# Eight experts instead of six norm their own rows in a hybrid encoder's mixture of experts; tiles, norms and slot finding placed elsewhere

## The chip, the core and the metric

The kernel is one program on one core of a Trainium2 chip. Its engines are TensorE (PE in the profile; PEld are its weight loads), VectorE (DVE), ScalarE (ACT), GpSimd (POOL) and SyncE (SP), each with its own queue of instructions that it works off in order; they meet through semaphores. SP and POOL issue the DMAs here. The metric is the device time of one execution in microseconds (us), lower is better.

## The reference

One layer of an encoder over 1024 tokens of width 1024: an input norm, one projection, three mixers side by side (retention, a state-space model, windowed attention), an output projection, a residual norm; then a mixture of experts and a last residual norm. The change lies in the last two:

```python
def expert_choice_ffn(x, router_w, w_gate, w_up, w_down):
    cap = EC_FACTOR * seq // N_EXPERTS                  # 128 tokens for each of 16 experts
    aff = jax.nn.softmax(einsum('bld,de->ble', x, router_w), axis=-1)
    gates, idx = lax.top_k(jnp.swapaxes(aff, 1, 2), cap)
    xs = x[bidx, idx]
    hdn = silu(xs @ w_gate) * (xs @ w_up)               # 1024 -> 2048, per expert
    out = (hdn @ w_down) * gates[..., None]             # 2048 -> 1024
    return jnp.zeros_like(x).at[bidx, idx].add(out)
h = layer_norm(ALPHA * h + expert_choice_ffn(h, ...), ln2_g, ln2_b)
```

Each expert takes its own 128 tokens, so a token can be in several experts or in none, and its row is complete when the last expert that has it has been added. Everything is float32; a product of two float32 operands is made of three matmuls on a high and a low part of each ("splits").

## The kernel before

**The expert stage.** Everything up to the router comes first; from about 505 us on, `Experts.quarter(q)` runs for q from 0 to 64. Expert e has the quarters 4e to 4e + 3, numbered f = 0 to 3. A quarter has six steps s, each one unit of weights of 1 MB: steps 0 and 1 multiply the tokens `xT` by a quarter of the gate matrix into `gu`, steps 2 and 3 by a quarter of the up matrix, and steps 4 and 5 multiply the hidden rows `hT` of the quarter before by the down matrix into `y`. A step is 12 matmuls on TensorE.

**The weights.** `load` (L1851) brings a unit from HBM into one of five raw buffers `wraw`; ScalarE rounds it to the high part of `whl` (L1858, `high`), VectorE subtracts that from the raw values to make the low part (L1865, `low`), which frees the raw buffer, and `low` at once issues the load of the unit five further on. After each step's matmuls the program has ScalarE and VectorE make the unit six steps ahead (`lead`), so both run some steps ahead of TensorE, but in program order with everything else on their queues.

**The hidden rows.** ScalarE takes the silu of the gate product after step 2 (L1894), VectorE multiplies by the up product after step 3 (L1900, `hid`), and TensorE transposes `hid` at the opening of the next quarter (L1803, `tp<-ident,hid`); ScalarE and VectorE split the result into `hT`. TensorE's transpose of `hid` thus stands behind every piece of work that VectorE has before L1900 in its queue.

**The order of the work around it** is written by hand. `at(self.before, q, s, fn)` and `at(self.after, q, s, fn)` hang a function before or after step s of quarter q; functions of one place run in the order in which they were hung there. `plan(q)` hangs those of quarter q, among them the slots and rows of the next expert: `expert_hot` (two comparisons on VectorE, L1770), `expert_slots` (eight small matmuls on TensorE, L1779), `expert_gather` (four tiny VectorE instructions and, issued by POOL, the gather `xs` of the expert's 128 rows from `h1_d`, L1792), and two halves of transposes of `xs`, split into `xT`.

**Summing and norming.** `acc_d` in HBM starts as the residual. The first experts, e < E - LAST, add their 128 rows to it with a scatter that adds (`expert_add`, L2022 and L2023). From e = E - LAST on, an expert gathers its rows of `acc_d` ahead (`final_rows`, L2041, into `eo`), adds its product to them on VectorE (`last_sum`, L2104), scatters the sums back (L2123), norms them (`last_mean` L2059 on ScalarE, L2060 on POOL; `last_var` L2066 on ScalarE, L2067 and L2068 on POOL; `last_gain` L2072 and `last_shift` L2076 on VectorE) and scatters them into the output (`last_scatter`, L2109); `last_norm` hangs this in the second quarter of the following expert, and expert 15 does it at the end (`last_rows`). For tokens that no such expert has, `final_norm` loads each of the eight tiles of 128 tokens of `acc_d` (`zz`, L2086 on SP), norms it with the same functions and stores it (L2089). Rows that an own-norm expert scatters later overwrite those of the tile; the order of the stores and scatters is kept by dependencies.

Of the kernel before, what the change touches and what calls it, by code (L numbers as in the profile page):

```python
# [20 lines left out]
P = 128  # L21
# [8 lines left out]
NEG = -1e30  # L30
TWO_PI = 6.283185307179586
PI_LO = 3.1415925
LAST = 6


def bcast(ap, n):
# [60 lines left out]
class Plan:  # L97
# [5 lines left out]
    def at(self, place, fn):  # L103
        self.items.append((place, len(self.items), fn))
# [1660 lines left out]
def expert_hot(K, e):  # L1765

    hot = []
    for t0 in range(0, NT, 4):
        hot.append(K.ex.tile([P, 4, P], BF16, name="hot", bufs=2))
        K.nc.vector.tensor_tensor(hot[-1], K.slot[:, t0:t0 + 4, e:e + 1].to_broadcast([P, 4, P]),  # L1770
                                  K.slots[:, None, :].to_broadcast([P, 4, P]), OP.is_equal)
    return hot


def expert_slots(K, e, hot):

    pt = K.ptp.tile([P, 4, P], F32, name="tp")
    for t in range(NT):
        K.nc.tensor.matmul(pt[:, 0, 0:5], hot[t // 4][:, t % 4, :], K.tok[:, t, e, :], start=(t == 0), stop=(t == NT - 1))  # L1779
    return pt  # L1780


def expert_gather(K, e, pt):

    nc, pool = K.nc, K.ex
    c = pool.tile([P, 6], F32, name="slotc", bufs=2)
    nc.vector.tensor_copy(c[:, 0:5], pt[:, 0, 0:5])
    nc.vector.tensor_tensor(K.index[:, e:e + 1], c[:, 0:1], c[:, 1:2], OP.add)
    xs = None
    if e:  # L1790
        xs = pool.tile([P, D], F32, name="xs", bufs=3)
        nc.gpsimd.indirect_dma_start(out=xs, out_offset=None, in_=K.h1_dram,  # L1792
                                     in_offset=bass.IndirectOffsetOnAxis(ap=K.index[:, e:e + 1], axis=0))
    nc.vector.tensor_tensor(c[:, 5:6], c[:, 3:4], c[:, 4:5], OP.add)
    nc.vector.tensor_tensor(K.gates[:, e:e + 1], c[:, 5:6], c[:, 2:3], OP.add)
    return xs
# [26 lines left out]
class Experts:  # L1823
# [59 lines left out]
    def plan(self, q):  # L1883

        K, nc, pool = self.K, self.K.nc, self.K.ex
        e, f = divmod(q, 4)
        at, box = self.at, {}

        def put(name, fn):
            return lambda: box.__setitem__(name, fn())  # L1890

        def silu():
            self.h[q] = pool.tile([P, 512], F32, name="hid", bufs=2)
            nc.scalar.activation(self.h[q], self.pg[q][0], AF.Silu)  # L1894

        def hidden():
            self.hT[q] = [pool.tile([P, 4, P], F32R, name=f"hT{s}", bufs=2) for s in range(2)]
            split(K, *self.hT[q], box["tp"])
        at(self.after, q, 2, silu)
        at(self.after, q, 3, lambda: nc.vector.tensor_tensor(self.h[q], self.h[q], self.pg[q][1], OP.mult))  # L1900
        s = 0 if q < 4 * E - 1 else 4
        at(self.before, q + 1, s, put("tp", lambda: turned(K, self.h[q], 0)))
        at(self.after if s == 0 else self.before, q + 1, s, hidden)
        if f == 0 and e + 1 < E:
            late = ((q, 0), (q, 3), (q, 3), (q + 2, 1)) if e else ((q + 2, 3), (q + 2, 4), (q + 2, 4), (q + 3, 3))
            at(self.after, *late[0], put("hot", lambda: expert_hot(K, e + 1)))
            at(self.before, *late[1], put("pt", lambda: expert_slots(K, e + 1, box["hot"])))
            at(self.after, *late[2], put("xs", lambda: expert_gather(K, e + 1, box["pt"])))
            for half in range(2):
                q1, s1 = late[3][0], late[3][1] + half  # L1910
                at(self.before, q1, s1, put(half, lambda half=half: turned(K, box["xs"], half * 4)))
                at(self.after, q1, s1, lambda half=half: self.tokens(e + 1, half, box[half]))
        if f == 0:
            if e < E - LAST:
                at(self.after, q + 5, 0, lambda: expert_add(K, e, self.py[e]))
            elif e < E - 1:
                last_norm(self, e)
        if q == 4 * (E - LAST):
            at(self.after, q, 1, lambda: final_consts(K, self.I))
            for t, n in enumerate((2, 3, 6, 10, 11, 14, 18, 22)):  # L1920
                final_norm(self, t, q + n)
        if q >= 4 * (E - LAST) and f == 0:
            at(self.after, q + 1, 3, lambda: final_rows(K, e))

# [132 lines left out]
def last_mean(K, z, junk, s):  # L2057

    K.nc.scalar.activation(junk, z, AF.Copy, accum_out=s[:, 0:1])  # L2059
    K.nc.gpsimd.tensor_scalar(s[:, 1:2], s[:, 0:1], -1.0 / D, None, op0=OP.mult)  # L2060


def last_var(K, z, junk, s):

    nc = K.nc
    nc.scalar.activation(junk, z, AF.Square, bias=s[:, 1:2], accum_out=s[:, 2:3])  # L2066
    nc.gpsimd.tensor_scalar(s[:, 3:4], s[:, 2:3], 1.0 / D, EPS, op0=OP.mult, op1=OP.add)  # L2067
    nc.gpsimd.tensor_tensor(s[:, 4:5], s[:, 3:4], K.mhalf[:, 0:1], OP.pow)  # L2068
# [10 lines left out]
def final_norm(X, t, q):  # L2079

    K, b = X.K, {}

    def load():
        zz = K.raw0.tile([P, 2, D], F32, name="zz", tag="wraw")
        b["z"], b["y"], b["s"] = zz[:, 0, :], zz[:, 1, :], stats_tile(K)
        K.nc.sync.dma_start(b["z"], K.acc_dram[t * P:(t + 1) * P, :])  # L2086

    def store():
        ins = K.nc.sync.dma_start(X.O["out"][t * P:(t + 1) * P, :], b["y"])  # L2089
        write_out(K, ins, K.scatters[-1:])  # L2090
        K.tiles.append(ins)
    X.at(X.after, q - 1, 5, load)
    X.at(X.after, q, 3, lambda: last_mean(K, b["z"], b["y"], b["s"]))
    X.at(X.after, q, 4, lambda: last_var(K, b["z"], b["y"], b["s"]))
    X.at(X.after, q + 1, 0, lambda: last_gain(K, b["z"], b["y"], b["s"]))
    X.at(X.after, q + 1, 1, lambda: last_shift(K, b["y"], b["s"]))
    X.at(X.after, q + 1, 2, store)


def last_sum(K, e, py, z):  # L2100
# [15 lines left out]
def last_norm(X, e):  # L2116

    K, b, q = X.K, {}, 4 * e + 5

    def total():  # L2120
        b["z"], b["s"] = K.last, stats_tile(K)
        last_sum(K, e, X.py[e], b["z"])
        K.nc.gpsimd.indirect_dma_start(out=K.acc_dram, in_=b["z"], in_offset=None,  # L2123
                                       out_offset=bass.IndirectOffsetOnAxis(ap=K.index[:, e:e + 1], axis=0))

    def mean():
        b["y"] = K.raw0.tile([P, 2, D], F32, name="yl", tag="wraw")[:, 0, :]
        last_mean(K, b["z"], b["y"], b["s"])

    def shift():  # L2130
        last_shift(K, b["y"], b["s"])
        last_scatter(K, X.O, e, b["y"])
    X.at(X.after, q, 0, total)
    X.at(X.after, q, 1, mean)
    X.at(X.after, q, 2, lambda: last_var(K, b["z"], b["y"], b["s"]))
    X.at(X.after, q, 3, lambda: last_gain(K, b["z"], b["y"], b["s"]))
    X.at(X.after, q, 4, shift)


def last_rows(X, e):  # L2140
# [205 lines left out]
```

## Time and profile before

| | us |
|---|---|
| timed runs | 1651.81, 1662.2, 4021.71; median 1662.2 |
| the profiled execution | 1650.03, of which the span from first to last instruction is 1648.3 |
| expert stage | from about 505 to the end |
| quarters 41 to 62, in which experts norm their own rows | from 1215.3 to 1613.2 |

The profile is of one execution on the core; its granted TensorE clock was 0.988 of full speed over the span. One of the timed runs (4021.71) lies far off the two others. A row of the order of time reads: start in us, how long, engine, line, operation, output <- inputs, and in brackets how long the engine was idle before and who ended that. In the rows a group of instructions has its count behind an x. Instructions that only issue a DMA or wait are not counted as busy.

### The profile page before, as it was taken

How to read it: one execution, taken by the hardware profiler on the slowest of the kernel's cores; microseconds unless marked ns; L12 is line 12 of the kernel's file. 1: busy time of each engine (PE TensorE's matmuls, PEld its weight loads, DVE VectorE, ACT ScalarE, POOL GpSimd, SP SyncE). 2: the span in 40 equal slices, each digit the busy share in tenths (PEclk: the TensorE clock that was granted, in tenths of full speed). 3: DMA queues.
4: the chain of work that ended last, by engine and by line, in shares of the span. 5: the costliest groups of instructions: out<-in, count | busy, mean ns of one | idle time of the engine just before them, and what ended most of it. 6: DMA issues, size and time to landing. Idle time of an engine off the chain costs nothing.

```text
span 1648.3 us, 21108 instructions
## 1 busy us (share of the span) xinstructions
PE 1571.1 (95%) x7704; PEld 1290.9 (78%) x7704; DVE 1415.7 (86%) x1734; ACT 1128.8 (68%) x1272; POOL 212.5 (13%) x237
## 2 busy tenths in 40 slices
PE   7999998899988999999999999999999999999997
PEld 5888887687776788888888888888887788777785
DVE  7986863777789989998898988989889998999996
ACT  4644544865746678777777777777768777786773
POOL 4002110011010010110101101011011304131221
PEclk9999999899999999999999999999999999999999
DMA  5566475425128999999999999999999999999993
GB/s 191 188 169 144 111 232 184 131 77 160 52 95 323 345 373 413 411 367 392 371 392 389 367 394 371 395 386 371 394 384 395 399 390 400 386 418 381 373 404 155
DMA packets 102682, 505.74 MB, mean 307 GB/s; under 512 B 12977, under 2 KB 28081, under 8 KB 51890
## 3 DMA queue, kind: packets, MB, share of 16 engines
q1 hardware_dynamic: 87426, 476.60, 75.3%
q0 software_dynamic: 15152, 27.79, 6.1%
q8 instruction: 60, 0.98, 0.2%
q14 instruction: 44, 0.36, 0.1%
HBM read 461.36 MB, written 42.99 MB: 306 GB/s over the span
## 4 chain that ended last, share of the span: by engine, by line
PE 61%; DVE 14%; DMA 10%; issue 7%; ACT 6%; POOL 1%; SPq 0%; POOLq 0%; DVEq 0%; ACTq 0%
PE gu L1818 26%; PE y L1818 13%; DVE whl L1865 6%; PE mm L79 4%; PE mm L81 4%; PE mm L80 4%; DMA zz<-acc_d 4%; DMA wraw<-in_exp_w_down 3%; ACT whl L1858 3%; DMA wraw<-in_exp_w_gate 2%; PE tp L1803 2%; PE po L1362 1%; ACT S L1336 1%; DVE pT L71 1%; PE sm L1462 1%
## 5 line engine op out<-in xcount | busy, mean ns | idle before, releaser
L1865 DVE TENSOR_TENSOR whl<-wraw,whl 128x2048 fp32r<-128x2048 f32 x384 | 873.0, 2288 | 90.4 <-ACT whl L1858 87.4
L1858 ACT ACTIVATE whl<-wraw 128x2048 fp32r<-128x2048 f32 x384 | 734.6, 1918 | 235.5 <-PE gu L1818 81.0
L1818 PE MATMUL gu<-whl,xT 128*128 128x512 f32 x3072 | 732.3, 395 | 0.0
L1818 PEld LDWEIGHTS gu<-whl,xT 128*128 128x128 f32 x3072 | 571.1, 189 | 117.2
L1818 PE MATMUL y<-whl,hT 128*128 128x512 f32 x1536 | 359.1, 389 | 0.7 <-ACT hT L70 0.7
L1818 PEld LDWEIGHTS y<-whl,hT 128*128 128x128 f32 x1536 | 288.2, 188 | 60.6 <-ACT hT L70 0.9
L1792 POOL DMA_INDIRECT xs<-h_d,index x15 | 41.4, 2759 | 732.7 <-PE y L1818 544.4
L79 PE MATMUL mm<-hT,whl 128*128 128x512 f32 x160 | 66.0, 412 | 0.0
L70 ACT ACTIVATE hT<-tp 128x512 fp32r<-128x512 f32 x80 | 45.9, 583 | 27.4 <-PE tp L178 14.1
L80 PE MATMUL mm<-hT,whl 128*128 128x512 f32 x160 | 62.7, 392 | 0.0
L81 PE MATMUL mm<-hT,whl 128*128 128x512 f32 x160 | 62.6, 391 | 0.0
L1803 PE MATMUL tp<-ident,hid 128*128 128x128 f32 x256 | 39.6, 278 | 21.3 <-DVE hid L1900 21.3
L71 DVE TENSOR_TENSOR hT<-tp,hT 128x512 fp32r<-128x512 f32 x80 | 54.0, 683 | 5.0 <-ACT hT L70 4.9
L1803 PEld LDWEIGHTS tp<-ident,hid 128*128 128x128 f32 x256 | 30.9, 141 | 33.5 <-DVE hid L1900 27.3
L79 PE MATMUL mm<-WO,yh 128*128 128x512 f32 x128 | 51.7, 404 | 3.4 <-ACT yh L70 3.4
L80 PE MATMUL mm<-WO,yh 128*128 128x512 f32 x128 | 50.3, 393 | 0.0
L81 PE MATMUL mm<-WO,yl 128*128 128x512 f32 x128 | 48.9, 392 | 0.0
L79 PE MATMUL mm<-whl,hT 128*128 128x512 f32 (+1 forms) x128 | 46.7, 365 | 0.1
L1336 ACT ACTIVATE S<-S,asm 128x384 f32<-128x384 f32 (+1 forms) x64 | 36.9, 578 | 13.0 <-DVE asm L1323 7.6
L81 PE MATMUL mm<-whl,hT 128*128 128x512 f32 (+1 forms) x128 | 44.3, 346 | 1.4 <-DVE hT L71 1.4
L80 PE MATMUL mm<-whl,hT 128*128 128x512 f32 (+1 forms) x128 | 44.4, 347 | 0.5 <-DVE whl L135 0.5
L1900 DVE TENSOR_TENSOR hid<-hid,gu 128x512 f32<-128x512 f32 x64 | 43.5, 680 | 1.1 <-PE gu L1818 1.0
(428 smaller groups left out, 1780.1 us busy)
## 6 DMA issues: line engine op xcount, KB each, us to landing
wraw<-in_exp_w_gate SPq DMA_DIRECT2D x128, 1024.0 KB, 7.9
wraw<-in_exp_w_up SPq DMA_DIRECT2D x128, 1024.0 KB, 8.0
wraw<-in_exp_w_down SPq DMA_DIRECT2D x128, 1024.0 KB, 8.3
wraw<-in_w_in SPq DMA_DIRECT2D x8, 1024.0 KB, 7.1
x<-in_x SPq DMA_DIRECT2D x8, 512.0 KB, 4.4
h_d<-x SPq DMA_DIRECT2D x8, 512.0 KB, 3.1
q_d<-kst SPq DMA_DIRECT2D x32, 128.0 KB, 2.5
wraw<-in_w_out SPq DMA_DIRECT2D x4, 1024.0 KB, 6.1
```

The costliest lines, as they stand in the source:

```text
L70: nc.scalar.activation(hi, src, AF.Copy)
L71: eng.tensor_tensor(lo, src, hi.bitcast(F32), OP.subtract)
L79: nc.tensor.matmul(ps, a[0], b[0], start=start, stop=False)
L80: nc.tensor.matmul(ps, a[0], b[1], start=False, stop=False)
L81: nc.tensor.matmul(ps, a[1], b[0], start=False, stop=stop)
L1336: nc.scalar.activation(S[g][:, :W], S[g][:, :W], AF.Exp, bias=nm[:, g:g + 1], accum_out=rs[:, g:g + 1])
L1792: nc.gpsimd.indirect_dma_start(out=xs, out_offset=None, in_=K.h1_dram, in_offset=bass.IndirectOffsetOnAxis(ap=K.index[:, e:e + 1], axis=0))
L1803: K.nc.tensor.transpose(pt[:, c, :], src[:, (c0 + c) * P:(c0 + c + 1) * P], K.ident)
L1818: nc.tensor.matmul(ps, a[s][c], u[:, t, i * w:(i + 1) * w], start=first and id(ps) not in began, stop=last and left[id(ps)] == 0)
L1858: self.K.nc.scalar.activation(u[:, 0, :], self.raw[k1].rearrange("p a b -> p (a b)"), AF.Copy)
L1865: self.K.nc.vector.tensor_tensor(u[:, 1, :], raw, u[:, 0, :].bitcast(F32), OP.subtract)
L1900: at(self.after, q, 3, lambda: nc.vector.tensor_tensor(self.h[q], self.h[q], self.pg[q][1], OP.mult))
```

## The change

Five things are done.

1. `LAST` goes from 6 to 8: experts 8 and 9 norm their own rows too, so eight do (8 to 15), and eight add (0 to 7).
2. The eight token tiles are normed one in each expert from 8 on, in its third and fourth quarters. Before, they stood at quarters 42, 43, 46, 50, 51, 54, 58 and 62 (two experts had two, and the adding ones none).
3. In each tile's norm the load moves from step 5 of the quarter before to step 0, the mean from step 3 to step 5, the variance from step 4 to step 0 of the next quarter, gain, shift and store one step later each.
4. In an own-norm expert's norm the mean goes from step 1 to 2, variance from 2 to 3, gain from 3 to 4, shift from 4 to 5.
5. Experts 1 to 7 find in their third quarter also the slots of expert e + 8 (9 to 15). Those experts' rows are then gathered (`expert_rows`, new) without the slot work in the quarter of the gather, at the place where they were gathered before.

```diff
-LAST = 6
+LAST = 8
...
+def expert_rows(K, e):
+
+    xs = K.ex.tile([P, D], F32, name="xs", bufs=3)
+    K.nc.gpsimd.indirect_dma_start(out=xs, out_offset=None, in_=K.h1_dram,
+                                   in_offset=bass.IndirectOffsetOnAxis(ap=K.index[:, e:e + 1], axis=0))
+    return xs
...
-    xs = None
-    if e:
-        xs = pool.tile([P, D], F32, name="xs", bufs=3)
...
+    xs = expert_rows(K, e) if rows else None
...
-            at(self.after, *late[0], put("hot", lambda: expert_hot(K, e + 1)))
-            at(self.before, *late[1], put("pt", lambda: expert_slots(K, e + 1, box["hot"])))
-            at(self.after, *late[2], put("xs", lambda: expert_gather(K, e + 1, box["pt"])))
+            if e < E - LAST:
+                at(self.after, *late[0], put("hot", lambda: expert_hot(K, e + 1)))
+                at(self.before, *late[1], put("pt", lambda: expert_slots(K, e + 1, box["hot"])))
+                at(self.after, *late[2], put("xs", lambda: expert_gather(K, e + 1, box["pt"], True)))
+            else:
+                at(self.after, *late[2], put("xs", lambda: expert_rows(K, e + 1)))
...
+        if f == 2 and 0 < e < E - LAST:
+            e2 = e + LAST
+            at(self.after, q, 0, put("hot", lambda: expert_hot(K, e2)))
+            at(self.before, q, 3, put("pt", lambda: expert_slots(K, e2, box["hot"])))
+            at(self.after, q, 3, lambda: expert_gather(K, e2, box["pt"]))
...
-            for t, n in enumerate((2, 3, 6, 10, 11, 14, 18, 22)):
-                final_norm(self, t, q + n)
+            for t in range(NT):
+                final_norm(self, t, q + 4 * t + 2)
...
-    X.at(X.after, q - 1, 5, load)
-    X.at(X.after, q, 3, lambda: last_mean(K, b["z"], b["y"], b["s"]))
-    X.at(X.after, q, 4, lambda: last_var(K, b["z"], b["y"], b["s"]))
-    X.at(X.after, q + 1, 0, lambda: last_gain(K, b["z"], b["y"], b["s"]))
-    X.at(X.after, q + 1, 1, lambda: last_shift(K, b["y"], b["s"]))
-    X.at(X.after, q + 1, 2, store)
+    X.at(X.after, q, 0, load)
+    X.at(X.after, q, 5, lambda: last_mean(K, b["z"], b["y"], b["s"]))
+    X.at(X.after, q + 1, 0, lambda: last_var(K, b["z"], b["y"], b["s"]))
+    X.at(X.after, q + 1, 1, lambda: last_gain(K, b["z"], b["y"], b["s"]))
+    X.at(X.after, q + 1, 2, lambda: last_shift(K, b["y"], b["s"]))
+    X.at(X.after, q + 1, 3, store)
...
-    X.at(X.after, q, 1, mean)
-    X.at(X.after, q, 2, lambda: last_var(K, b["z"], b["y"], b["s"]))
-    X.at(X.after, q, 3, lambda: last_gain(K, b["z"], b["y"], b["s"]))
-    X.at(X.after, q, 4, shift)
+    X.at(X.after, q, 2, mean)
+    X.at(X.after, q, 3, lambda: last_var(K, b["z"], b["y"], b["s"]))
+    X.at(X.after, q, 4, lambda: last_gain(K, b["z"], b["y"], b["s"]))
+    X.at(X.after, q, 5, shift)
```

**VectorE in the quarter where an expert's rows are summed and normed.** Names: `whl<-wraw,whl` is a low part, `eo<-y,gates,eo` the sum, `hT` the hidden rows' low part, `yl<-eo,fst,gb` the gain, `yl<-yl,fst,gb` the shift, `hid` the product that TensorE transposes next. Before:

```order
L2104 SCALAR_TENSOR_TENSOR eo<-y,gates,eo 128x512 x2
L71 TENSOR_TENSOR hT_11166<-tp,hT_11165 128x512
L1865 TENSOR_TENSOR whl<-wraw,whl 128x2048 x3
L2072 SCALAR_TENSOR_TENSOR yl<-eo,fst,gb_10517 128x1024
L1900 TENSOR_TENSOR hid<-hid,gu 128x512
L1865 TENSOR_TENSOR whl<-wraw,whl 128x2048
L2076 SCALAR_TENSOR_TENSOR yl<-yl,fst,gb_10517 128x1024
L1865 TENSOR_TENSOR whl<-wraw,whl 128x2048 x2
```

Of the kernel with the change, the same quarter:

```order
L2116 SCALAR_TENSOR_TENSOR eo<-y,gates,eo 128x512 x2
L71 TENSOR_TENSOR hT_10233<-tp,hT_10232 128x512
L1869 TENSOR_TENSOR whl<-wraw,whl 128x2048 x3
L1904 TENSOR_TENSOR hid<-hid,gu 128x512
L1869 TENSOR_TENSOR whl<-wraw,whl 128x2048
L2084 SCALAR_TENSOR_TENSOR yl<-eo,fst,gb_9627 128x1024
L1869 TENSOR_TENSOR whl<-wraw,whl 128x2048
L2088 SCALAR_TENSOR_TENSOR yl<-yl,fst,gb_9627 128x1024
```

The gain has moved from ahead of `hid` to one low part behind it, the shift follows one low part later.

**ScalarE in the third quarter of an own-norm expert, where a token tile is normed.** `whl<-wraw` is a high part, `hid<-gu` the silu, `zz,fst<-zz` the mean, `zz,fst<-zz,fst` the variance, `hT<-tp` the hidden rows' high part at the opening of the next quarter. Before:

```order
L1894 ACTIVATE hid<-gu 128x512
L1858 ACTIVATE whl<-wraw 128x2048
L2059 ACTIVATE zz,fst<-zz 128x1024
L1858 ACTIVATE whl<-wraw 128x2048
L2066 ACTIVATE zz,fst<-zz,fst 128x1024
L1858 ACTIVATE whl<-wraw 128x2048 x2
L70 ACTIVATE hT_11433<-tp 128x512
```

Of the kernel with the change:

```order
L1898 ACTIVATE hid<-gu 128x512
L1862 ACTIVATE whl<-wraw 128x2048 x3
L2071 ACTIVATE zz,fst<-zz 128x1024
L1862 ACTIVATE whl<-wraw 128x2048
L2078 ACTIVATE zz,fst<-zz,fst 128x1024
L70 ACTIVATE hT_10499<-tp 128x512
```

The mean stands two high parts later in the quarter, and the variance directly ahead of `hT`; its load is issued one step later than it was.

**VectorE in the third quarter of an adding expert**, where the slots of a later expert are now found (`hot` are the comparisons, `xT` the next expert's tokens, `slotc`, `index` and `gates` the slot numbers). Of the kernel with the change; in the kernel before, the rows with `hot`, `slotc`, `index` and `gates` are not in this quarter:

```order
L1770 TENSOR_TENSOR hot<-slot,slots 128x512 x2
L1869 TENSOR_TENSOR whl<-wraw,whl 128x2048
L71 TENSOR_TENSOR xT_8845<-tp,xT_8844 128x512
L1869 TENSOR_TENSOR whl<-wraw,whl 128x2048
L71 TENSOR_TENSOR xT_8845<-tp,xT_8844 128x512
L1869 TENSOR_TENSOR whl<-wraw,whl 128x2048
L1904 TENSOR_TENSOR hid<-hid,gu 128x512
L1795 COPY slotc<-tp 128x5
L1796 TENSOR_TENSOR index<-slotc 128x1
```

Two comparisons have come to stand ahead of this quarter's `hid`, the tiny ones behind it.

More of the change, by code (lines that the diff above doesn't have):

```diff
@@ L1780, in expert_slots, with expert_gather @@
     return pt
-def expert_gather(K, e, pt):
+def expert_rows(K, e):
[3 more added lines that the diff above has]
+    return xs
+def expert_gather(K, e, pt, rows=False):
     nc, pool = K.nc, K.ex
@@ L1788, in expert_gather @@
     nc.vector.tensor_tensor(K.index[:, e:e + 1], c[:, 0:1], c[:, 1:2], OP.add)
-    xs = None
-    if e:
-        xs = pool.tile([P, D], F32, name="xs", bufs=3)
-        nc.gpsimd.indirect_dma_start(out=xs, out_offset=None, in_=K.h1_dram,
-                                     in_offset=bass.IndirectOffsetOnAxis(ap=K.index[:, e:e + 1], axis=0))
+    xs = expert_rows(K, e) if rows else None
     nc.vector.tensor_tensor(c[:, 5:6], c[:, 3:4], c[:, 4:5], OP.add)
```

## The prediction

> **What bounds the kernel now.** I read the page first, then the engines by stretch, then TensorE's own order of time, then who waits for whom where TensorE stops.
>
> ```profile
> PE 1571.1 (95%) x7704; PEld 1290.9 (78%) x7704; DVE 1415.7 (86%) x1734; ACT 1128.8 (68%) x1272; POOL 212.5 (13%) x237
> ```
>
> TensorE is busy 95% of the span, so little is left to win anywhere. The change touches only the expert stage, from about 505 us on. Busy time by stretch (us, then PE, PEld, DVE, ACT, POOL, granted clock, DMA share, GB/s), one stretch of the experts that add their rows, two of those that norm their own, and two short ones:
>
> ```profile
> 860.00:960.00 100.00, 100.00 (x470) 82.40 (x469) 89.37 (x61) 74.64 (x53) 9.89 (x4) 1.00 0.98 378
> 1284.00:1353.00 69.00, 66.95 (x306) 54.66 (x305) 65.79 (x46) 50.74 (x40) 15.71 (x10) 0.98 0.99 393
> 1353.00:1421.00 68.00, 64.87 (x297) 53.15 (x296) 61.99 (x42) 54.55 (x46) 21.86 (x13) 1.00 1.00 396
> 1440.00:1450.00 10.00, 10.00 (x46) 8.29 (x45) 8.61 (x7) 7.86 (x8) 4.26 (x4) 1.00 1.02 428
> 1450.00:1460.00 10.00, 7.99 (x42) 6.39 (x41) 10.00 (x7) 7.70 (x7) 4.88 (x2) 1.00 1.01 424
> ```
>
> In the adding experts TensorE has no gap. In the own-norm experts it has, VectorE stands near 95%, and DMA moves 393 to 396 GB/s on average and up to 428 over 10 us. TensorE's transposes of `hid` open every quarter (a quarter is a fourth of an expert), so their starts are a ruler; the bracket is idle time before them:
>
> ```profile
> 1078.13 0.60 PE L1803 MATMUL tp<-ident,hid 128*128 128x128 f32 x4
> 1094.95 0.60 PE L1803 MATMUL tp<-ident,hid 128*128 128x128 f32 x4
> 1112.75 0.60 PE L1803 MATMUL tp<-ident,hid 128*128 128x128 f32 x4
> 1146.71 0.60 PE L1803 MATMUL tp<-ident,hid 128*128 128x128 f32 x4
> 1215.29 0.60 PE L1803 MATMUL tp<-ident,hid 128*128 128x128 f32 x4
> 1306.92 0.66 PE L1803 MATMUL tp<-ident,hid 128*128 128x128 f32 x4 [2.04 <-DVE hid L1900]
> 1378.29 0.66 PE L1803 MATMUL tp<-ident,hid 128*128 128x128 f32 x4 [1.03 <-DVE hid L1900]
> 1452.72 0.66 PE L1803 MATMUL tp<-ident,hid 128*128 128x128 f32 x4 [2.01 <-DVE hid L1900]
> 1524.50 0.66 PE L1803 MATMUL tp<-ident,hid 128*128 128x128 f32 x4 [2.00 <-DVE hid L1900]
> 1596.35 0.66 PE L1803 MATMUL tp<-ident,hid 128*128 128x128 f32 x4 [0.99 <-DVE hid L1900]
> 1613.21 0.60 PE L1803 MATMUL tp<-ident,hid 128*128 128x128 f32 x4
> ```
>
> The last opens quarter 63 (the one after, 64, has only the down projection). Counting back, 1215.29 opens quarter 41, 1146.71 quarter 37 and 1078.13 quarter 33. An expert without gaps takes 1146.71 - 1078.13 = 68.58 us, a quarter 17.145 on average; its second quarter takes 16.82 and its third, with the transposes of `xs`, 17.80. From quarter 33 to 63, 30 quarters, the kernel takes 535.1 us where 30 × 17.145 = 514.4 would do. So **20.7 us** is all that this change can win, 1.3% of the profiled execution's 1650.0 us. Who is waited for there (us in total, times, longest):
>
> ```profile
> ACT zz L2059 <- DMA zz<-acc_d: 20.1, 8, 4.1
> PE tp L1803 <- DVE hid L1900: 15.6, 12, 2.2
> PE tp L1779 <- DVE hot L1770: 2.0, 4, 0.7
> ```
>
> TensorE's gaps are waits for `hid` (15.6) and for the slots' `hot` (2.0): VectorE is late. The five gaps listed above, 8.1 us together, are those at the end of the quarter in which an expert's rows are summed and normed. Inside one of them, VectorE's and ScalarE's order of time:
>
> ```profile
> 1440.70 1.40 DVE L2104 SCALAR_TENSOR_TENSOR eo<-y,gates,eo 128x512 f32<-128x512 f32 x2
> 1442.14 1.06 ACT L2059 ACTIVATE yl<-eo 128x1024 f32<-128x1024 f32 x1 [2.96 <-DVE eo L2104]
> 1445.13 2.29 DVE L1865 TENSOR_TENSOR whl<-wraw,whl 128x2048 fp32r<-128x2048 f32 x1 [0.23 <-ACT whl L1858]
> 1448.58 2.29 DVE L1865 TENSOR_TENSOR whl<-wraw,whl 128x2048 fp32r<-128x2048 f32 x1 [1.16 <-ACT whl L1858]
> 1450.79 1.28 DVE L2072 SCALAR_TENSOR_TENSOR yl<-eo,fst,gb 128x1024 f32<-128x1024 f32 x1
> 1451.99 0.68 DVE L1900 TENSOR_TENSOR hid<-hid,gu 128x512 f32<-128x512 f32 x1
> ```
>
> ScalarE stands 2.96 us at the row's mean because VectorE has not summed yet, so its next splits come late, VectorE waits 0.23 and 1.16 for them, then does the gain (1.28), and only then `hid`, for which TensorE has stood 2.01.
>
> **The change part by part.** Prices, from the groups by line (busy us, mean ns) and the DMA issues (KB, us to landing):
>
> ```profile
> L71 DVE TENSOR_TENSOR xT<-tp,xT 128x512 fp32r<-128x512 f32 x31 | 21.2, 683 | 1.4 <-ACT xT L70 1.4
> L1770 DVE TENSOR_TENSOR hot<-slot,slots 128x512 bf16<-128x512 f32 x30 | 19.2, 682 | 0.0
> L2072 DVE SCALAR_TENSOR_TENSOR zz<-zz,fst,gb 128x1024 f32<-128x1024 f32 x8 | 10.2, 1278 | 0.0
> L2104 DVE SCALAR_TENSOR_TENSOR eo<-y,gates,eo 128x512 f32<-128x512 f32 x12 | 8.4, 744 | 4.9 <-PE y L1818 4.9
> L2041 POOL DMA_INDIRECT eo<-acc_d,index x6 | 11.6, 1928 | 29.8 <-DMA acc_d<-eo,index 13.2 <-issue 13.1 <-PE y L1818 3.5
> L2109 POOL DMA_INDIRECT out<-yl,index x6 | 25.8, 4306 | 12.9 <-DVE yl L2076 11.3 <-DVE yl L62 1.6
> zz<-acc_d SPq DMA_DIRECT2D x8, 512.0 KB, 9.7
> wraw<-in_exp_w_gate SPq DMA_DIRECT2D x128, 1024.0 KB, 7.9
> ```
>
> *The row norm one step later.* The mean goes from step 1 to step 2, the variance to 3, the gain to 4, behind `hid`, the shift to 5. On the path of the example 0.23 + 1.16 + 1.28 = 2.67 us go against a gap of 2.01: the gap closes with 0.66 to spare. The gain and shift are not saved, they now stand between this `hid` and the next. In that third quarter VectorE has six splits of 2.29, gain and shift 2.56, and four pieces of 0.68 (`hT`, two `xT`, `hid`), 19.0; neighbours overlap by 0.08 each (the gain above ends at 1452.07, `hid` begins at 1451.99), 13 times, which leaves 18.0 against TensorE's 17.80: late by 0.2 in each of seven quarters, 1.4 us.
>
> *Token tiles.* Each tile's load goes to step 0 of an expert's third quarter and its mean to step 5: five steps where there were four. A step is 17.145 / 6 = 2.86 us, and a load lands 9.7 us after its issue; ScalarE runs ahead of TensorE, so four steps (11.4) were not enough and five (14.3) should be. ScalarE's wait for `zz` (20.1 over 8, longest 4.1) shrinks by 2.86 each time, to about 1 us in all. Tiles no longer come in successive quarters (they did twice), and an own-norm expert has one where it had 8/6.
>
> *Slots.* The `hot` comparisons and small slot products of experts 9 to 15 go into the third quarters of experts 1 to 7. TensorE does as many of them as before, and its 2.0 us of waits for `hot` go. What they push there: a base quarter's own end, VectorE's `hid` and TensorE's use of it:
>
> ```profile
> 1041.09 0.68 DVE L1900 TENSOR_TENSOR hid<-hid,gu 128x512 f32<-128x512 f32 x1
> 1044.17 0.60 PE L1803 MATMUL tp<-ident,hid 128*128 128x128 f32 x4
> ```
>
> `hid` is there 2.4 us early, and two `hot` cost 1.36: hidden. Without that cover it would be up to 1.4 us in each of seven quarters, 10 us; below nothing it cannot go. I take 0.5 us in all.
>
> *VectorE in sum.* An adding expert takes 0.894 × 68.58 = 61.3 us of it. An own-norm expert had 61.3 + 1.5 (two sums) + 2.56 + 8/6 × 2.56 = 68.8, more than TensorE's 68.58. Now it has 61.3 - 1.4 + 1.5 + 2 × 2.56 = 66.5. Experts 8 and 9 become own-norm experts and rise to that, below the bound too.
>
> *Traffic.* Experts 8 and 9 gain a gather and an output scatter each, 4 × 0.52 = 2.1 MB, and 4 issues on POOL's queue (1.93 and 4.31 us each), where nothing critical stands behind them: the next row gather is half an expert from its use. An own-norm expert moves 24 × 1.049 + 6 × 0.524 = 28.3 MB, in 68.58 us 413 GB/s. The two short stretches show 424 and 428, so it can be had, but its second quarter carries three of the six extra transfers: 6.29 + 1.57 = 7.86 MB, at 426 GB/s 18.5 us where TensorE needs 16.82. Of that lag of 1.6 the spare 0.66 takes a part; I charge 1.0 in each of seven quarters, 6.8 us, between nothing (the ring of raw weights absorbs it all) and 1.6 × 7 = 11. The Trainium skill, "DMA: Bandwidth & Descriptors", section "Where 436 GB/s comes from", lets the HBM side bind such transfers at about 358 GB/s per core. By that page an own-norm expert would take 79 us and the kernel about 1708. The trace disagrees: 378 to 396 GB/s over 68 to 100 us, so I give it no chance of its own.
>
> *First own-norm quarters.* The two constants of 0.5 MB are loaded at the start of expert 8 instead of 10. The quarters after them showed one gap:
>
> ```profile
> 1250.63 0.66 PE L1803 MATMUL tp<-ident,hid 128*128 128x128 f32 x4 [0.56 <-DVE hid L1900]
> ```
>
> I allow the same, 0.6 us. The tail behind the last product is not touched.
>
> **Sum.** -20.7 + 1.4 + 6.8 + 0.6 + 0.5 = -11.4, from 1650.0 to 1638.6. The lowest timed run lies 1.8 above the profiled one (1651.8), the median 1662.2 another 10; I forecast on the side of the undisturbed ones: 1640.
>
> **The rivals.**
> - *DMA becomes the bound, slower.* Own-norm work now fills quarters 33 to 62, 7.5 experts of 28.3 MB, 212 MB. If the engines give over the whole stretch only what they gave from 1284 to 1353, 393 GB/s, it takes 540.2 us instead of 535.1: 1655.1, timed about 1657. It decides below 212.3 / 535.1 = 397 GB/s. For it: both own-norm stretches shown stay below it at a DMA share of 0.99 and 1.00. Against: in those stretches VectorE's lateness held back the loads, which are issued when a split frees a buffer.
> - *All gaps go*: 1650.0 - 20.7 + 0.5 = 1629.8, timed 1632, if the ring absorbs the bursts. For it: adding experts run without a gap at a DMA share of 0.98.
> - *A new wait in place of the old.* Gain and shift of the tile now stand close before `hid` in the fourth quarter, after a third that leaves no spare. The gaps outside the five listed are 15.6 - 8.1 = 7.5 us; if they stay, 1638.6 + 7.5 = 1646, timed 1648.
> - *POOL's added work blocks VectorE.* Two gathers, two scatters, 12.5 us. If VectorE stood as long, less 2.1 us of room in each of experts 8 and 9, 8.3 us would be lost: 1647, timed 1649. The row against it, three splits beside a gather being issued:
>
> ```profile
> 1288.28 6.70 DVE L1865 TENSOR_TENSOR whl<-wraw,whl 128x2048 fp32r<-128x2048 f32 x3
> 1288.37 3.14 POOL L1792 DMA_INDIRECT xs<-h_d,index  x1 [16.13 <-DVE gates L1795]
> ```
>
> 2.23 us each, no slower than alone. "SBUF — State Buffer" of the Trainium skill, section "Who interferes with whom", says that a VectorE instruction with two inputs in SBUF contends with a GpSimd instruction that reads SBUF, one of them blocking fully. By that, this rival would hold; on the VectorE side the trace does not show it here.
>
> **How the numbers follow.** Chances: forecast 0.52 (1635 to 1645 timed), DMA the bound 0.17, new wait 0.14, all gaps gone 0.13, POOL 0.04. The range takes in the floor less a little and the DMA rival: 1629 to 1658. A measurement of this kernel tells about 2% from no change, some 33 us; no case reaches that, and only the floor, timed against a median that is itself 10 us high, would come near it. Faster 0.04, within 0.94, slower 0.02.
>
> **What would show it.** In the profile after: TensorE without a wait of 2 us for `hid` at the end of second quarters; ScalarE's wait for `zz` below 5 us in total; no wait of TensorE for `hot` late; the ruler from quarter 33 to 63 near 524 us; own-norm stretches above 400 GB/s. If they stay below 397 with ScalarE waiting longer for weights, the DMA rival is right. If `hid` is late after fourth quarters, the new wait is. If `hid` is late in third quarters of experts 1 to 7, the price of the slots was wrong.

## The result, and the profile after

The changed kernel takes 1635.2 us in the median of six runs (1627.3 to 1638.7); the kernel before, with three runs more, 1652.5. The ratio is **0.989, 95% interval 0.985 to 0.994**: faster, by less than the 2% that counts as told apart. The profiled executions took 1636.5 and 1650.0 us, 13.5 apart, where the forecast's sum had 11.4.

The first part of the page, and the engines by stretch (one stretch of adding experts, two of own-norm ones; the columns are those of before):

```profile
PE 1568.8 (96%) x7704; PEld 1290.4 (79%) x7704; DVE 1418.9 (87%) x1742; ACT 1130.8 (69%) x1276; POOL 210.1 (13%) x247
```

```profile
860.00:960.00 100.00, 100.00 (x477) 82.22 (x476) 91.62 (x67) 75.11 (x53) 9.90 (x4) 1.00 0.98 375
1290.00:1360.00 70.00, 69.73 (x320) 57.36 (x319) 67.03 (x43) 55.79 (x44) 12.51 (x10) 1.00 1.01 413
1360.00:1430.00 70.00, 69.88 (x322) 57.57 (x321) 66.23 (x41) 55.70 (x43) 14.75 (x10) 1.00 1.01 414
```

An adding expert's VectorE went from 89% to 92%: the slots are found there now. The own-norm stretches hold TensorE busy to over 99%, VectorE is busy 96% and 95% of them (before 95% and 91%, where the prediction reads "near 95%" for both), and DMA moves 413 GB/s where it moved 393 to 396. The ruler, TensorE's transposes of `hid`:

```profile
893.77 0.60 PE L1807 MATMUL tp<-ident,hid 128*128 128x128 f32 x4
911.91 0.60 PE L1807 MATMUL tp<-ident,hid 128*128 128x128 f32 x4
...
1083.38 0.60 PE L1807 MATMUL tp<-ident,hid 128*128 128x128 f32 x4
...
1151.63 0.60 PE L1807 MATMUL tp<-ident,hid 128*128 128x128 f32 x4
1168.45 0.60 PE L1807 MATMUL tp<-ident,hid 128*128 128x128 f32 x4
1186.26 0.60 PE L1807 MATMUL tp<-ident,hid 128*128 128x128 f32 x4
1204.70 0.66 PE L1807 MATMUL tp<-ident,hid 128*128 128x128 f32 x4 [1.47 <-DVE hid L1904]
...
1275.06 0.66 PE L1807 MATMUL tp<-ident,hid 128*128 128x128 f32 x4 [1.80 <-DVE hid L1904]
...
1599.92 0.60 PE L1807 MATMUL tp<-ident,hid 128*128 128x128 f32 x4
```

1083.38 opens quarter 33 and 1599.92 quarter 63, **516.5 us** instead of 535.1. An own-norm expert's second quarter (1151.63 to 1168.45) takes 16.82 and its third 17.81, as without norms. The two largest gaps, 1.47 and 1.80, stand at the end of fourth quarters. A third quarter of an adding expert (893.77 to 911.91) takes 18.14, where it took 17.80. The waits from 1080 us on (us in total, times, longest):

```profile
PE tp L1807 <- DVE hid L1904: 3.9, 4, 1.8
```

ScalarE's wait for `zz`'s load, 20.1 us before, does not appear among the waits any more, and TensorE waits for `hid` 3.9 us instead of 15.6. VectorE inside a second quarter, and TensorE's use of its `hid`:

```profile
1435.45 1.40 DVE L2116 SCALAR_TENSOR_TENSOR eo<-y,gates,eo 128x512 f32<-128x512 f32 x2
1436.77 0.68 DVE L71 TENSOR_TENSOR hT<-tp,hT 128x512 fp32r<-128x512 f32 x1
1437.36 6.69 DVE L1869 TENSOR_TENSOR whl<-wraw,whl 128x2048 fp32r<-128x2048 f32 x3
1443.97 0.68 DVE L1904 TENSOR_TENSOR hid<-hid,gu 128x512 f32<-128x512 f32 x1
1444.57 2.29 DVE L1869 TENSOR_TENSOR whl<-wraw,whl 128x2048 fp32r<-128x2048 f32 x1
1446.03 0.60 PE L1807 MATMUL tp<-ident,hid 128*128 128x128 f32 x4
1446.77 1.28 DVE L2084 SCALAR_TENSOR_TENSOR yl<-eo,fst,gb 128x1024 f32<-128x1024 f32 x1
```

From the sum to `hid` VectorE no longer stops, the gain stands behind `hid`, and `hid` (done at 1444.65) is 1.4 us early.

### The profile page after: what moved, and what is told of

It is laid out like the page before. It is cut to its first block, busy times and chain, and to the rows that moved or that the text cites. A ratio compares the mean times of both kernels' runs of the same rounds, so it can differ in the third digit from the quotient of the medians.

```text
span 1634.6 us, 21145 instructions
## 1 busy us (share of the span) xinstructions
PE 1568.8 (96%) x7704; PEld 1290.4 (79%) x7704; DVE 1418.9 (87%) x1742; ACT 1130.8 (69%) x1276; POOL 210.1 (13%) x247
## 4 chain that ended last, share of the span: by engine, by line
PE 49%; DVE 22%; DMA 14%; issue 8%; ACT 5%; POOL 1%; SPq 0%; POOLq 0%; DVEq 0%; ACTq 0%
PE gu L1822 19%; DVE whl L1869 11%; PE y L1822 9%; DMA wraw<-in_exp_w_down 8%; PE mm L79 4%; PE mm L81 4%; PE mm L80 4%; DMA wraw<-in_exp_w_up 4%; ACT whl L1862 2%; DMA wraw<-in_exp_w_gate 2%; DVE hT L71 1%; PE po L1362 1%; PE tp L1807 1%; DVE hid L1904 1%; DVE pT L71 1%
## 5 line engine op out<-in xcount | busy, mean ns | idle before, releaser
L1869 DVE TENSOR_TENSOR whl<-wraw,whl 128x2048 fp32r<-128x2048 f32 x384 | 870.9, 2286 | 70.2 <-ACT whl L1862 68.1
L1786 POOL DMA_INDIRECT xs<-h_d,index x15 | 30.0, 1999 | 461.0 <-PE y L1822 301.4
L1807 PEld LDWEIGHTS tp<-ident,hid 128*128 128x128 f32 x256 | 31.3, 141 | 20.1 <-DVE hid L1904 13.1
```

Source lines behind the costliest of these rows:

```text
L1786: K.nc.gpsimd.indirect_dma_start(out=xs, out_offset=None, in_=K.h1_dram, in_offset=bass.IndirectOffsetOnAxis(ap=K.index[:, e:e + 1], axis=0))
L1807: K.nc.tensor.transpose(pt[:, c, :], src[:, (c0 + c) * P:(c0 + c + 1) * P], K.ident)
L1869: self.K.nc.vector.tensor_tensor(u[:, 1, :], raw, u[:, 0, :].bitcast(F32), OP.subtract)
```

## The experiments

In each run the ruler is read from quarter 33 to 63, where experts norm their rows, and from 5 to 33, the adding ones. Quarters 5 to 33 are the same program in all runs that find the slots early; six of these eight took 482.1 to 482.6 us there, the changed kernel 483.0 with 0.5 us of TensorE's waits for `hot`, undo_tile_step 485.4 with 2.4. Why the waits fell into these two stays open. The six runs that find the slots late all took 480.1. From 33 to 63 the two profiles of the changed kernel differ by 2.4 us; the others were profiled once, so differences of 2 to 3 us there say little. "VectorE" is the work per own-norm expert by the prediction's prices; what the traces show for it comes with only_steps.

The granted TensorE clock has a part in these numbers. Some quarters that open with a stop of 1.9 us or more have a mean clock of 0.91 to 0.92 and take some 1.6 us longer without any idle time, while others behind such a stop run at 1.00. The loss stands at their start: in the one shown below the clock is 0.50 from 1346.9 to 1349, 0.68 to 1351 and 1.00 from there. From 33 to 63 there is one such quarter each in the kernel before, only_steps, level_only, undo_slots and undo_norm_step, three in only_norm_step, four in only_eight, and none in the changed kernel, after_again, tile_behind, undo_tile_step, steps_no_tile_gain and extra1. One of only_norm_step (a first quarter, 17.15 us without a gap):

```profile
1346.90:1365.66 18.76, 18.76 (x84) 15.35 (x85) 17.90 (x15) 12.48 (x8) 1.68 (x1) 0.91 1.00 405
```

| run | VectorE, us | order of norm / tile | 5 to 33 | 33 to 63 | sum |
|---|---|---|---|---|---|
| before | 68.8 | old / old | 480.1 | 535.1 | 1015.2 |
| only_norm_step | 68.8 | new / old | 480.1 | 536.1 | 1016.2 |
| only_steps | 68.8 | new / new | 480.1 | 530.1 | 1010.2 |
| only_eight | 67.9 | old / old | 480.1 | 539.6 | 1019.7 |
| undo_slots | 67.9 | new / new | 480.1 | 526.7 | 1006.8 |
| level_only | 66.5 | old / old | 482.6 | 530.6 | 1013.2 |
| undo_norm_step | 66.5 | old / new | 482.4 | 529.5 | 1011.9 |
| undo_tile_step | 66.5 | new / old | 485.4 | 520.8 | 1006.1 |
| changed kernel | 66.5 | new / new | 483.0 | 516.5 | 999.5 |
| after_again | 66.5 | new / new | 482.2 | 514.1 | 996.3 |
| steps_no_tile_gain | 65.4 | new / old | 480.1 | 517.6 | 997.7 |

**undo_norm_step.** The own-norm experts' steps are put back:

```diff
-    X.at(X.after, q, 2, mean)
-    X.at(X.after, q, 3, lambda: last_var(K, b["z"], b["y"], b["s"]))
-    X.at(X.after, q, 4, lambda: last_gain(K, b["z"], b["y"], b["s"]))
-    X.at(X.after, q, 5, shift)
+    X.at(X.after, q, 1, mean)
+    X.at(X.after, q, 2, lambda: last_var(K, b["z"], b["y"], b["s"]))
+    X.at(X.after, q, 3, lambda: last_gain(K, b["z"], b["y"], b["s"]))
+    X.at(X.after, q, 4, shift)
```

> The changed kernel with one part undone: in an own-norm expert's norm the mean, variance, gain and shift stand at steps 1, 2, 3, 4 again. Theory (the order on VectorE and ScalarE ahead of hid): the gaps of TensorE at the end of second quarters come back, five of them were 8.1 us before, so about 1.6 us in each of seven, and quarters 33 to 63 take 516.5 + 11 = 527 us or so. Rival (the relief came from the traffic, spread more evenly over eight experts): nothing in the traffic changes, so 516.5 within 2 us and no gap over 1 us at the end of second quarters. Second rival (the sum of VectorE's work per expert, not its order): the work is the same, so 516.5 within 2 us too.

The ruler at quarters 33 and 63, and the wait:

```profile
1081.47 0.60 PE L1807 MATMUL tp<-ident,hid 128*128 128x128 f32 x4
...
1610.98 0.60 PE L1807 MATMUL tp<-ident,hid 128*128 128x128 f32 x4
```

```profile
PE tp L1807 <- DVE hid L1904: 14.0, 11, 3.1
```

529.5 us, 13 to 15 more than with the new steps, at the same traffic and the same sum of work. Order it is, in this setting.

**undo_tile_step.** The tiles' steps are put back (load at step 5 of the quarter before, then 3, 4, 0, 1, 2):

```diff
-    X.at(X.after, q, 0, load)
-    X.at(X.after, q, 5, lambda: last_mean(K, b["z"], b["y"], b["s"]))
-    X.at(X.after, q + 1, 0, lambda: last_var(K, b["z"], b["y"], b["s"]))
...
+    X.at(X.after, q - 1, 5, load)
+    X.at(X.after, q, 3, lambda: last_mean(K, b["z"], b["y"], b["s"]))
+    X.at(X.after, q, 4, lambda: last_var(K, b["z"], b["y"], b["s"]))
...
```

> The changed kernel with one part undone: a token tile's load stands at step 5 of the quarter before, its mean at step 3, the variance at 4, gain, shift and store at 0, 1, 2 of the next quarter, as before; there is still one tile in each expert. Theory: ScalarE waits for zz again, about 2.5 us for each of eight tiles, 20 us in all, and VectorE's splits come late behind it; the gaps outside the second quarters were 7.5 us before, of which about half should come back: 518 to 523 us for quarters 33 to 63. If the wait for zz cost nothing, 516.5 within 1 us, or less, since gain and shift stand two steps further from the hid behind them.

```profile
1083.90 0.60 PE L1807 MATMUL tp<-ident,hid 128*128 128x128 f32 x4
...
1604.66 0.60 PE L1807 MATMUL tp<-ident,hid 128*128 128x128 f32 x4
```

```profile
ACT zz L2071 <- DMA zz<-acc_d: 22.5, 8, 3.4
```

520.8 us. The wait for `zz` is back in full, 22.5 us of ScalarE. The old steps cost 4 to 7 us; gain and shift moved with the load and the mean, so this is not the wait's price alone.

**undo_slots.** Experts 9 to 15 find their slots when they are due:

```diff
-            if e < E - LAST:
-                at(self.after, *late[0], put("hot", lambda: expert_hot(K, e + 1)))
...
-            else:
-                at(self.after, *late[2], put("xs", lambda: expert_rows(K, e + 1)))
+            at(self.after, *late[0], put("hot", lambda: expert_hot(K, e + 1)))
+            at(self.before, *late[1], put("pt", lambda: expert_slots(K, e + 1, box["hot"])))
+            at(self.after, *late[2], put("xs", lambda: expert_gather(K, e + 1, box["pt"], True)))
...
-        if f == 2 and 0 < e < E - LAST:
...
```

> The changed kernel with one part undone: the slots of experts 9 to 15 are found in experts 8 to 14 again, in the quarter of the gather. Theory (order): TensorE's waits for hot come back, 0.5 us in each of seven experts, and the small matmuls' 0.33 us with them, so 516.5 + 3.5 + 2.3 = 522 us for quarters 33 to 63, while quarters 5 to 33 fall by 2.3 from 483.0 to about 480.5; the end is 1 to 4 us later. Rival (the sum of VectorE's work): an own-norm expert rises from 66.5 to 67.9 us of VectorE against 68.6 of TensorE, waits included it is then the bound, and the gaps before hid return at 1 us or more per expert, 525 us or more.

```profile
1079.54 0.60 PE L1807 MATMUL tp<-ident,hid 128*128 128x128 f32 x4
...
1606.23 0.60 PE L1807 MATMUL tp<-ident,hid 128*128 128x128 f32 x4
```

```profile
PE tp L1807 <- DVE hid L1904: 10.2, 7, 2.3
```

526.7 us; some 2.3 of the 10 to 13 more are the small matmuls, which move along. The rest comes back as waits for `hid` (10.2, where the changed kernel has 2.0 to 3.9) and one quarter at the lower clock, not as waits for `hot`, so it is VectorE's added work and not TensorE's wait for the slots: the rival of the sum is right here. All seven gaps stand at the end of fourth quarters, while the comparisons stand in first quarters, behind the `hid` that is late (at 1420.30 us, where that `hid` ran at 1412.49): what is added in one quarter is paid for in another. 1.4 us of VectorE per expert, with the tiny instructions, cost about 9 us in seven experts.

**only_norm_step.** The kernel before with the first diff above the other way round, nothing else.

> The kernel before with one part of the change alone: the mean, variance, gain and shift of an own-norm expert stand one step later (2, 3, 4, 5). Six experts still norm their own rows, the tiles and slots are where they were. Theory (order): the five gaps of 8.1 us at the end of second quarters go, quarters 33 to 63 take 527 us instead of 535.1. Rivals (traffic, or the sum of VectorE's work): neither changes, so 535 within 2 us, with the gaps moved to other quarters.

```profile
1081.51 0.60 PE L1803 MATMUL tp<-ident,hid 128*128 128x128 f32 x4
...
1309.35 0.66 PE L1803 MATMUL tp<-ident,hid 128*128 128x128 f32 x4 [1.69 <-DVE hid L1900]
1346.90 1.11 PE L1803 MATMUL tp<-ident,hid 128*128 128x128 f32 x4 [2.35 <-DVE hid L1900]
...
1565.78 1.11 PE L1803 MATMUL tp<-ident,hid 128*128 128x128 f32 x4 [2.52 <-DVE hid L1900]
...
1617.62 0.60 PE L1803 MATMUL tp<-ident,hid 128*128 128x128 f32 x4
```

536.1 us: nothing gained, and the theory of order alone fell. Without the three quarters at the lower clock, and the one before, it would be 531.6 against 533.5, an estimate from the lengths of those quarters. Of the five gaps at the end of second quarters two stay (1.69 is one), three close, and others open behind: 2.35 stands at the end of a fourth quarter that had no gap before, and the 2.52 was 2.18 there.

**level_only and only_eight.** The changed kernel with both step parts undone, and the kernel before with `LAST = 8` and one tile in each own-norm expert alone:

```diff
-LAST = 6
+LAST = 8
...
-            for t, n in enumerate((2, 3, 6, 10, 11, 14, 18, 22)):
-                final_norm(self, t, q + n)
+            for t in range(NT):
+                final_norm(self, t, q + 4 * t + 2)
```

> The changed kernel with both step parts undone: experts' rows normed at steps 1 to 4, tiles loaded at step 5 and normed at 3, 4, 0, 1; eight own-norm experts, one tile in each and the slots found early stay. The three runs before leave two theories. Theory A (VectorE's work per own-norm expert first: 68.8 us in the kernel before, the bound itself, 66.5 here; order second): the levelling alone brings part of the gain, quarters 33 to 63 take 530 to 534 us (undoing the one step part cost 13.0 and the other 4.3, which add to 516.5). Theory B (order is the bulk, levelling only matters through it): all of the gain is gone, 535 or more.

```profile
1078.48 0.60 PE L1807 MATMUL tp<-ident,hid 128*128 128x128 f32 x4
...
1609.07 0.60 PE L1807 MATMUL tp<-ident,hid 128*128 128x128 f32 x4
```

> The kernel before with eight own-norm experts and one tile in each, and nothing else: norms and tiles at their old steps, slots found late. VectorE's work per own-norm expert is 61.3 + 1.5 + 5.1 = 67.9 us, against 68.8 before, but in eight experts. If the costs of the undone parts add (10.2 + 13.0 + 4.3 on 516.5), quarters 33 to 63 take 544 us, 9 more than before. If the traffic's even spread is what helps, 530 or less. If the parts overlap (a gap that one causes covers the other's), 532 to 538.

```profile
1078.06 0.60 PE L1803 MATMUL tp<-ident,hid 128*128 128x128 f32 x4
...
1617.61 0.60 PE L1803 MATMUL tp<-ident,hid 128*128 128x128 f32 x4
```

Levelling without order: 530.6, where theory A said 530 to 534 for quarters 33 to 63 and B 535 or more. But 2.3 of the 4.5 us less are the small matmuls, which stand in the adding experts now: from quarter 5 to 63 it gains 2.0, hardly more than two profiles of one kernel differ. Eight own-norm experts alone: 539.6, 4.5 more than before and between the two forecasts (532 to 538 if the costs of the undone parts overlap, 544 if they add); its four quarters at the lower clock, instead of one, are about 5 us. So the traffic's even spread is not what helps, and the costs do not add in full.

**only_steps and steps_no_tile_gain.** Both are the kernel before with the norm's new steps. The first has the tiles' new steps too; the second has the old ones, with the tiles' gain and shift left out:

```diff
-    X.at(X.after, q + 1, 0, lambda: last_gain(K, b["z"], b["y"], b["s"]))
-    X.at(X.after, q + 1, 1, lambda: last_shift(K, b["y"], b["s"]))
```

> The kernel before with both step parts of the change (experts' rows at steps 2 to 5; tiles loaded at step 0, normed at 5, 0, 1, 2) and without the levelling: six own-norm experts, two of them with two tiles, slots found late. Theory (VectorE's work per own-norm expert is a bound of its own, 68.8 us here): the new order finds no room, quarters 33 to 63 stay at 533 to 537 us, although ScalarE no longer waits for zz. Rival (the tiles' late load spoilt the run with the norm's step alone): 524 us or less.

```profile
1077.96 0.60 PE L1803 MATMUL tp<-ident,hid 128*128 128x128 f32 x4
...
1608.08 0.60 PE L1803 MATMUL tp<-ident,hid 128*128 128x128 f32 x4
```

> The kernel before with the experts' rows normed one step later, and the token tiles' gain and shift left out (their stored rows are not the normed ones): VectorE has 8/6 x 2.56 = 3.4 us less per own-norm expert, 65.4 instead of 68.8, while traffic, tile places and everything else are those of the run that had the norm's step alone and took 536.1 us. Theory (VectorE's sum): quarters 33 to 63 fall to 516 to 522 us. Rival (traffic of 8/6 tiles and of the late zz loads is what binds): 532 us or more.

```profile
1079.79 0.60 PE L1803 MATMUL tp<-ident,hid 128*128 128x128 f32 x4
...
1597.40 0.60 PE L1803 MATMUL tp<-ident,hid 128*128 128x128 f32 x4
```

```profile
PE tp L1803 <- DVE hid L1900: 1.7, 4, 1.1
```

Order without levelling gives 530.1: 5.0 us less than before, between the two readings (533 to 537, or 524 and less). Taking 3.4 us of VectorE's work per expert out of only_norm_step brings it from 536.1 to 517.6, with the same traffic, the same places of tiles, and ScalarE's wait for `zz` still there (21.4 us in its waits). Some 4.5 of these 18.5 us are the three quarters at the lower clock, which it does not have. So neither the traffic nor the wait for `zz` alone closed the way in the kernel before, but the tiles' gain and shift had a large part in it. The run takes away their work and, for six of eight tiles, their place ahead of a fourth quarter's `hid` at once, so it does not part the sum from the order. Order gives 5.0 us from quarter 5 to 63, levelling 2.0, both together 15.7 to 18.9.

What each does shows on VectorE itself. Over experts 11 to 14, from the opening of quarter 45 to that of 61 (the busy times of all engines, then VectorE's wait for ScalarE's high parts), first before, then after:

```profile
1287.88:1578.39 290.51, 277.54 (x1274) 226.57 (x1273) 270.52 (x185) 219.60 (x172) 70.85 (x43) 0.99 1.00 395
DVE whl L1865 <- ACT whl L1858: 19.6, 22, 2.6
1291.94:1566.29 274.35, 273.55 (x1249) 225.33 (x1248) 261.61 (x161) 218.96 (x169) 53.63 (x39) 1.00 1.01 412
DVE whl L1869 <- ACT whl L1862: 12.4, 14, 1.5
```

| run | these four experts, us | VectorE busy | VectorE waits for high parts |
|---|---|---|---|
| before | 290.5 | 270.5 | 19.6 |
| only_norm_step | 293.4 | 270.5 | 22.3 |
| only_steps | 287.6 | 271.9 | 13.3 |
| level_only | 284.7 | 262.6 | 21.5 |
| undo_norm_step | 282.3 | 261.5 | 20.6 |
| undo_slots | 282.1 | 267.9 | 13.6 |
| changed kernel | 274.3 | 261.6 | 12.4 |

Nearly all of VectorE's idle time ends on a high part of ScalarE. Levelling takes down VectorE's work, the two step parts together take down its waits, and neither of them does the other's; only with both do work and wait come down to 274.0 us, beside the 273.5 that TensorE is busy. The norm's step alone leaves the waits where they were, with the wait for `zz` still there (22.4 us of ScalarE).

**after_again and tile_behind.** The changed kernel once more, and with the tiles' gain, shift and store behind the fourth quarter's `hid`:

```diff
-    X.at(X.after, q + 1, 1, lambda: last_gain(K, b["z"], b["y"], b["s"]))
-    X.at(X.after, q + 1, 2, lambda: last_shift(K, b["y"], b["s"]))
-    X.at(X.after, q + 1, 3, store)
+    g = [(q + 1, 4), (q + 1, 5), (q + 2, 0)] if t < NT - 1 else [(q + 1, 1), (q + 1, 2), (q + 1, 3)]
+    X.at(X.after, *g[0], lambda: last_gain(K, b["z"], b["y"], b["s"]))
+    X.at(X.after, *g[1], lambda: last_shift(K, b["y"], b["s"]))
+    X.at(X.after, *g[2], store)
```

> The changed kernel once more, to see how far its profile repeats: 516.5 within 2 us for quarters 33 to 63, and 483 within 2 us for quarters 5 to 33, which other kernels with the same program there showed at 482.4 and 485.4.

```profile
1082.16 0.60 PE L1807 MATMUL tp<-ident,hid 128*128 128x128 f32 x4
...
1596.24 0.60 PE L1807 MATMUL tp<-ident,hid 128*128 128x128 f32 x4
```

> The changed kernel with the tiles' gain, shift and store moved behind hid of the fourth quarter: steps 4 and 5, and step 0 of the next expert's first quarter (the last tile stays). Theory (order): the gaps that are left, 4.0 us before hid at the end of fourth quarters, go, since the first quarter of an expert now has the least work on VectorE; quarters 33 to 63 take 512 to 513 us, 4 us less than the changed kernel. Rival (they come from loads that land late): 516 within 1.5 us.

```profile
1080.90 0.60 PE L1807 MATMUL tp<-ident,hid 128*128 128x128 f32 x4
...
1594.54 0.60 PE L1807 MATMUL tp<-ident,hid 128*128 128x128 f32 x4
```

```profile
PE tp L1807 <- DVE hid L1904: 0.9, 3, 0.4
```

The changed kernel repeats at 514.1, a little outside the 2 us allowed, with 2.0 us of TensorE's waits for `hid` instead of 3.9. Timed in the same rounds its ratio is 0.988 (0.986 to 0.990), that of tile_behind 0.988 (0.985 to 0.990): medians 1633.6 and 1632.0. The fourth quarters' gaps are gone in tile_behind (0.9 us of waits are left, at the end of second quarters), which bears out where they came from, but the 4 us expected of it are not there: 513.6 against 516.5 and 514.1 is no gain that these runs can tell.

**extra1 and extra3.** One and three loads of 0.5 MB more beside each tile's:

```diff
+        for i in range(1):
+            K.nc.sync.dma_start(b["y"], K.h1_dram[(t + i) % NT * P:((t + i) % NT + 1) * P, :])
         K.nc.sync.dma_start(b["z"], K.acc_dram[t * P:(t + 1) * P, :])
```

> The changed kernel with one more load of 0.5 MB beside each tile's load (rows that are overwritten unread), so 28.8 MB per own-norm expert instead of 28.3. Theory (the DMA engines can give 426 GB/s, the room that the forecast's traffic charge was taken from): 28.8 / 0.426 = 67.7 us, still below 68.6, so quarters 33 to 63 take 515 us, up to 518. Rival (the 411 GB/s that the changed kernel shows is already their limit): 28.8 / 0.411 = 70.1 us per expert, 526 us.

```profile
1081.90 0.60 PE L1807 MATMUL tp<-ident,hid 128*128 128x128 f32 x4
...
1601.15 0.60 PE L1807 MATMUL tp<-ident,hid 128*128 128x128 f32 x4
```

519.2 us, between the two: 3 to 5 us more than the changed kernel's two profiles, 1.2 above the theory's upper end and 7 below the rival. So 411 GB/s is not the limit. ScalarE waits 3.8 us for `zz` again, so whether the bytes or the later `zz` cost the time stays open.

> The changed kernel with three more loads of 0.5 MB beside each tile's load, 29.9 MB per own-norm expert. Theory (limit at 426 GB/s): 70.2 us per expert of DMA, 1.6 above TensorE, so quarters 33 to 63 take 527 us, up to 532 with the three loads bunched in one place. Rival (limit at 411): 72.7 us per expert, 545 us. If neither binds (the limit is higher than the trace has shown): 516.

```profile
1083.04 0.60 PE L1807 MATMUL tp<-ident,hid 128*128 128x128 f32 x4
...
1673.32 0.60 PE L1807 MATMUL tp<-ident,hid 128*128 128x128 f32 x4
```

```profile
SPq L2099 <- DMA zz<-h_d: 97.3, 16, 10.1
```

590.3 us, above all three forecasts, but not by traffic: the three loads go to one place, so SP waits for each to land before it issues the next (97.3 us over 16 waits, 6 each), and the weight loads stand behind it. The run says nothing of the DMA engines' limit, which stays open. It does price a wait at that place of SP's queue.

## Why the prediction was right

The time (1635.2 against 1640), the side and the mechanism came out; several terms were mis-sized, and one step failed. That the profiled 1636.5 lies so near to the sum's 1638.6 is in part luck: 8.8 us of charges that did not fall due (third quarters, traffic, constants) stand against 3.9 us of gaps in fourth quarters that were left out, 2.9 lost in the adding experts where 0.5 was charged, and 2.4 before quarter 5; with the 2.3 us of small matmuls that left the own-norm stretch the sum would be 1636.2.

- *Row norm one step later.* As forecast, no gap is left at the end of second quarters: 1.4 us to spare where 0.66 was worked out. **What failed is that this step's gain was taken by itself.** The sum let its gaps close as if the room it makes were kept. Alone it gave nothing (536.1 against 535.1): gaps closed in some quarters and opened in others. The working had VectorE at 68.8 us per expert, more than TensorE's 68.58, as a sum beside the terms and not as a condition for them. The trace puts that sum right: before, VectorE was busy 67.6 us in each of experts 11 to 14 (270.5 / 4) and waited 4.9 for ScalarE's high parts, 72.5 of the 72.6 that such an expert took. Its work alone would have fitted; with the waits beside it, it did not. With the levelling in, the step is worth 13 to 15 us.
- *Third quarters* were charged 1.4 us and cost nothing: 17.81 us.
- *Token tiles.* The wait for `zz` went from 20.1 to none, where about 1 was forecast. Undone, it costs 4 to 7 us.
- *Slots.* From quarter 33 on TensorE no longer waits for `hot`, and 0.5 us was charged to the adding experts, which lost 2.9. 0.5 of that are waits for `hot` in the first two of them, not late `hid`, and some 2.3 the small matmuls, 0.33 us in each of seven third quarters (18.14 against 17.80), and the own-norm stretch is shorter by as much: moved, not added, but the ruler should have been shifted for it. What the part is worth, about 9 us by undo_slots, is VectorE's relief, and the prediction priced only the 2.0 us of waits.
- *Traffic* was charged 6.8 us and cost close to nothing: second quarters took 16.82 us with all their transfers, at 413 GB/s over 70 us. By that the ring of raw weights absorbs the burst, the lower of the two ends given.
- *Constants*, 0.6 charged: no gap there.
- *Fourth quarters* were charged nothing in the sum. The rival "a new wait in place of the old" named their place and gave 7.5 us; 3.9 came in one profile and 2.0 in the other, and tile_behind takes them away. So that rival was half there beside the forecast.
- *DMA as the bound*: its point was 397 GB/s, and the stretches show 413 and 414. *POOL's work blocking VectorE*: with 10 POOL instructions more, the splits take 2286 ns on average where they took 2288:

```profile
L1869 DVE TENSOR_TENSOR whl<-wraw,whl 128x2048 fp32r<-128x2048 f32 x384 | 870.9, 2286 | 70.2 <-ACT whl L1862 68.1
```

The over-charged terms (1.4 + 6.8 + 0.6) and the fourth quarters that were left out (-3.9), with the small matmuls' shift, account for a ruler of 516.5 instead of some 523. Of what the ruler gained over the forecast, 2.4 us are lost up to quarter 5 (reached at 600.4 instead of 598.0), where the program is the same; between the profiles of all these kernels that point lies anywhere from 595.9 to 601.4.

## What to carry to other kernels

Before pricing a wait by itself, add up each engine's work per period in the stretch and the waits that it keeps beside it: where the two fill the period, closing one of its gaps only moves it; here the same reordering gave nothing at 68.8 us of VectorE's work and 13 to 15 at 66.5, beside 68.6 of TensorE's. In a hand-ordered queue, what a neighbour waits for belongs ahead of what nobody waits for, and work with no fixed place belongs into the periods that have room; here either alone gave 2 to 5 us and both 16 to 19. A ruler made of an instruction that recurs in every period shows a few microseconds that the times of whole runs cannot, and beside the gaps themselves it shows the quarters that a lower clock made longer.

## What the runs showed that was not expected

- Two changes that gave 5.0 and 2.0 us gave 15.7 to 18.9 together.
- Behind some of TensorE's stops of 1.9 us or more the granted clock was low for some 4 us (0.50, then 0.68, in the stretches named above), and the quarter took about 1.6 us longer on top of the stop.
- DMA held 413 to 414 GB/s over 70 us with gathers, scatters and stores among the loads, where the kernel before showed 393 to 396 in such stretches. With the old traffic and less work on VectorE (steps_no_tile_gain) the stretches of 120 to 130 us from 1220 on show 407 to 420, so the DMA engines had not been the limit.
- Three loads into one place kept SP's queue for about 6 us at each wait, and cost 9 us per expert, (590.3 - 516.5) / 8 tiles; the same bytes spread out would be 1.6 MB beside 28.3.
